# High and low weight matmuls that take turns in a column tile of a two-layer hybrid encoder

## The chip, the cores and the metric

One core of one Trainium2 chip runs the whole program in one launch. The metric is the device time of one execution in microseconds (us), the median of several runs. TensorE is called PE here, its weight loads PEld, VectorE DVE, ScalarE ACT, GpSimd POOL and SyncE SP, as in the profile.

## The reference, cut to what matters

Two layers over 256 positions of width 2048, all float32. Each layer normalises the stream, makes one large projection, feeds four mixers (A short convolution, B attention, C a scan in two directions, D a long convolution), projects each mixer back, merges them with sigmoid gates and projects once more:

```
h = rms_norm(x, norm_g)
proj = h @ w_in                       # 2048 x (13*512 + 256 + 4*2048)
ya, yb, yc, yd = mixers(split_cols(proj))
bp = einsum('bskc,kcd->bskd', stack(ya, yb, yc, yd), w_branch)
merged = sum(sigmoid(gates + b_gate) * bp, axis=2)
x = x + merged @ w_out
```

The matrices w_in, w_branch and w_out carry nearly all the arithmetic, and they are what the change touches.

## The kernel before, in words

**The weight stream.** Weights come from HBM in chunks of 128 x 1024 float32 (512 KB), 306 a layer, 612 in all, in the order of the list `STREAM` (line 90). SP loads a chunk into a `raw` buffer (`load`, line 410). ACT rounds it to a type that PE multiplies in one pass, which gives `hi` (`fetch`, line 420), and DVE subtracts, raw minus hi, which gives `lo` (`low`, line 435). There are four `raw`, three `hi` and two `lo` buffers. `chunk` (line 442) hands out the next chunk and, in program order, asks ACT for the hi two chunks ahead and DVE for the lo one chunk ahead. Both carry high priority with the scheduler. With two lo buffers, the lo of the next chunk can be written only when the last lo matmul of the chunk before this one has been done; with three hi buffers, a hi cast waits for the last hi matmul three chunks earlier.

**A column tile.** `tile_b` (line 475) makes 128 output columns for all 256 positions from two chunks, so 137 tiles a layer are 274 chunks a layer. The activations are kept split too: each operand tile is [128, 4, 2, 256], where the axis of 2 holds the high and the low part. For each chunk `wide` (line 464) makes eight matmuls with a 128x128 piece of hi against both activation parts (512 columns, into both halves of a PSUM bank) and eight with the same piece of lo against the high part alone (256 columns, into the first half). The other 32 chunks a layer belong to the branch projections; they go through `tile_branch` and `passes` (line 452), which the change leaves alone. So there are 137 x 2 x 8 x 2 layers = 4384 pairs of a hi and a lo matmul in `wide`.

**Side work between the matmuls.** The mixers are generators. After each matmul (or pair) `pump` (line 348) is called. It looks at a model clock, `now`, that each emitted matmul moves on, and emits the next step of every generator that is due, PE work on `sd` PSUM tiles included. PE's order is thus written out by the program and kept as it stands; DVE and ACT are ordered by a scheduler. Nearly all instructions are recorded at line 201, a helper, so the groups of the profile are told apart by the names of their tiles: `mg` and `mb` are PSUM banks of the weight stream, `sd` those of side work, `slab` the activation operands.

Of the kernel before, what the change touches and what calls it, by code (L numbers as in the profile page):

```python
# [211 lines left out]
class Kern:  # L212
# [250 lines left out]

    def wide(self, o, w, xs, first, last):

        nc = self.nc
        hi, lo = w
        for i, (c, x) in enumerate(xs):
            nc.tensor.matmul(o, hi[:, c * P:(c + 1) * P], x, start=first and i == 0, stop=False)
            self.pump()  # L470
        for i, (c, x) in enumerate(xs):
            nc.tensor.matmul(o[:, 0], lo[:, c * P:(c + 1) * P], x[:, 0, :], start=False, stop=last and i == len(xs) - 1)
            self.pump()

# [1039 lines left out]
```

## Time and profile before

| | |
|---|---|
| median of 3 runs | 1971.63 us (1971.6 to 1974.53) |
| the profiled execution's own time | 1974.37 us |
| its span, first to last instruction | 1972.3 us |
| mean granted TensorE clock | 0.994 |
| PE busy | 1924.5 us (98% of the span) |
| DVE busy | 1443.4 us (73%) |
| ACT busy | 1260.6 us (64%) |

Of the profiled execution 2.1 us lie outside the span, and it is 2.7 us longer than the median. Matmuls are pipelined, and the length that a record shows includes that of the pipeline; what a matmul costs in a row of matmuls is read from the distance between starts.

### The profile page before, as it was taken

The page shows a single profiled execution, that of the slowest core. Times are in us where ns is not written, and L with a number is a line of the kernel's source. Part 1 is how long each engine was busy: PE and PEld are TensorE (multiplying, and loading weights), DVE is VectorE, ACT ScalarE, POOL GpSimd, SP SyncE. Part 2 cuts the span into 40 slices and gives each one's busy share as a digit, 9 for nine tenths or more (in the row PEclk, how much of TensorE's full clock was granted, in tenths as well). Part 3 has the DMA queues.
Part 4 walks back from the last instruction along what each step waited for, and adds up shares of the span by engine and source line. Part 5 has one row for each costly group of instructions (what it writes and reads, how often), then busy time and mean ns, then how long its engine had stood idle before and what let it go on. Part 6 is the DMA issues. An engine that isn't in the chain of part 4 may idle for free.

```text
span 1972.3 us, 32350 instructions
## 1 busy us (share of the span) xinstructions
PE 1924.5 (98%) x12190; PEld 1703.6 (86%) x12190; DVE 1443.4 (73%) x2496; ACT 1260.6 (64%) x2292; POOL 71.1 (4%) x117
## 2 busy tenths in 40 slices
PE   8999999999999999999999999999999999999997
PEld 6888878898898998898888888888988889989886
DVE  7777969977788566666687679799677966565665
ACT  6677666767647776554466766776765577655544
POOL 1001010000001000000000010000001000000000
PEclk9999999999999999999999999999999999999998
DMA  7555544454565445666665555544555554465653
GB/s 249 175 169 171 164 154 144 145 168 161 169 198 171 150 150 178 201 193 216 213 191 176 176 171 163 157 149 143 176 165 179 176 178 150 152 208 196 201 184 128
DMA packets 97692, 343.17 MB, mean 174 GB/s; under 512 B 11808, under 2 KB 12192, under 8 KB 97536
## 3 DMA queue, kind: packets, MB, share of 16 engines
q1 hardware_dynamic: 93312, 331.48, 51.4%
q0 software_dynamic: 3648, 8.59, 1.8%
q8 instruction: 95, 1.56, 0.3%
q10 hardware_dynamic: 576, 1.05, 0.1%
q14 instruction: 61, 0.50, 0.1%
HBM read 332.48 MB, written 8.39 MB: 173 GB/s over the span
## 4 chain that ended last, share of the span: by engine, by line
PE 92%; DVE 6%; issue 1%; ACT 1%; DMA 0%; DVEq 0%; SPq 0%; ACTq 0%
PE mg L201 73%; PE mb L201 9%; PE sd L201 9%; DVE arena L201 3%; DVE lo L201 2%; DVE slab L201 1%; DMA arena<-xT 0%; DVE part L201 0%; DVE bdE L201 0%; ACT L175 0%; ACT arena L201 0%; ACT slab L201 0%; ACT bdE L201 0%; DVEq L1509 0%; ACT part L201 0%
## 5 line engine op out<-in xcount | busy, mean ns | idle before, releaser
L201 PE MATMUL mg<-slab,hi 128*128 128x512 f32 x4368 | 1144.3, 398 | 12.6 <-DVE slab L201 12.5
L201 DVE TENSOR_TENSOR lo<-raw,hi 128x1024 fp32r<-128x1024 f32 x612 | 747.8, 1222 | 361.6 <-PE mg L201 286.3
L201 ACT ACTIVATE hi<-raw 128x1024 fp32r<-128x1024 f32 x612 | 646.5, 1057 | 459.5 <-PE mg L201 319.5
L201 PEld LDWEIGHTS mg<-slab,hi 128*128 128x128 f32 x4368 | 781.5, 190 | 155.9 <-DVE slab L201 16.0
L201 PEld LDWEIGHTS mg<-slab,lo 128*128 128x128 f32 x4368 | 602.1, 190 | 46.0 <-issue 2.8
L201 PE MATMUL mg<-slab,lo 128*128 128x256 f32 x4368 | 635.3, 285 | 0.0
L201 DVE TENSOR_TENSOR arena<-arena 128x512 f32<-128x512 f32 (+17 forms) x390 | 165.3, 432 | 11.6 <-DMA arena<-scratch 3.5
L201 DVE SCALAR_TENSOR_TENSOR arena<-arena,par 128x256 f32<-128x256 f32 x346 | 153.1, 477 | 4.4 <-ACT arena L201 3.1
L201 PE MATMUL mb<-slab,hi 128*128 128x256 f32 (+1 forms) x1040 | 153.6, 288 | 0.0
L201 DVE TENSOR_TENSOR arena<-mg,arena 128x256 f32<-128x256 f32 x305 | 127.4, 418 | 16.0 <-ACT arena L201 10.8
L201 PEld LDWEIGHTS mb<-slab,hi 128*128 128x128 f32 x1040 | 137.2, 192 | 1.0
L201 ACT ACTIVATE arena<-arena,b_gate 128x256 f32<-128x256 f32 x128 | 64.8, 506 | 79.2 <-DVE arena L201 78.8
L201 ACT ACTIVATE arena<-arena 128x256 f32<-128x256 f32 (+4 forms) x194 | 93.5, 497 | 13.2 <-DVE arena L201 12.6
L201 ACT ACTIVATE arena<-mg 128x256 f32<-128x256 f32 x241 | 89.4, 371 | 7.6 <-PE mg L201 4.9
L201 PE MATMUL mb<-slab,lo 128*128 128x256 f32 x528 | 88.1, 287 | 0.0
L175 ACT ACT_TABLE_LOAD x62 | 79.5, 1283 | 9.5 <-PE sd L201 7.0
L201 DVE SCALAR_TENSOR_TENSOR arena<-arena,mb 128x512 f32<-128x512 f32 x64 | 43.8, 684 | 47.5 <-PE mb L201 46.3
L201 PEld LDWEIGHTS mb<-slab,lo 128*128 128x128 f32 x528 | 74.5, 193 | 0.3
L201 ACT ACTIVATE bdE<-sd 64x128 f32<-64x128 f32 x256 | 62.9, 268 | 8.3 <-PE sd L201 6.0
L201 ACT ACTIVATE arena<-sd 128x64 f32<-128x64 f32 (+4 forms) x122 | 40.2, 331 | 23.3 <-PE sd L201 21.7
L201 ACT ACTIVATE arena<-arena,par 128x256 f32<-128x256 f32 x88 | 41.2, 508 | 6.4 <-DVE arena L201 5.9
L201 PE MATMUL sd<-arena 96*128 96x256 f32 (+3 forms) x224 | 43.8, 338 | 0.9 <-DVE arena L201 0.9
(96 smaller groups left out, 1021.3 us busy)
## 6 DMA issues: line engine op xcount, KB each, us to landing
raw<-w SPq DMA_DIRECT2D x612, 512.0 KB, 3.4
arena<-xT SPq DMA_DIRECT2D x4, 512.0 KB, 8.2
scratch<-slab POOLq DMA_DIRECT2D x16, 128.0 KB, 3.0
scratch<-arena POOLq DMA_DIRECT2D x8, 256.0 KB, 4.3
arena<-xT SPq DMA_DIRECT2D x8, 256.0 KB, 3.9
x<-arena SPq DMA_DIRECT2D x8, 256.0 KB, 3.9
arena<-x SPq DMA_DIRECT2D x8, 256.0 KB, 4.3
arena<-lorab POOLq DMA_DIRECT2D x16, 96.0 KB, 3.1
```

What stands on the lines that cost most here:

```text
L175: return f(out)
L201: return f(out, *args, **kw)
```

## The change

In `wide` the second loop is gone. Each pass of the one loop that is left makes the hi matmul of a piece and then its lo matmul, and calls `pump` once behind the pair, not once behind each matmul. The number and the sizes of the matmuls are the same, `start` still stands on the first hi matmul of a tile and `stop` on its last lo matmul.

```diff
         for i, (c, x) in enumerate(xs):
             nc.tensor.matmul(o, hi[:, c * P:(c + 1) * P], x, start=first and i == 0, stop=False)
-            self.pump()
-        for i, (c, x) in enumerate(xs):
             nc.tensor.matmul(o[:, 0], lo[:, c * P:(c + 1) * P], x[:, 0, :], start=False, stop=last and i == len(xs) - 1)
             self.pump()
```

On PE, at the first chunk of the first column tile (`mg_209` is its PSUM bank, `hi_128` and `lo_130` the two parts of the chunk, `slab_106` and `slab_107` the operands), before:

```order
L201 MATMUL mg_209<-slab_106,hi_128 128x512 x4
L201 MATMUL mg_209<-slab_107,hi_128 128x512 x4
L201 MATMUL mg_209<-slab_106,lo_130 128x256 x4
L201 MATMUL mg_209<-slab_107,lo_130 128x256 x4
L201 MATMUL mg_209<-slab_108,hi_148 128x512 x4
L201 MATMUL mg_209<-slab_109,hi_148 128x512 x4
```

And with the change, the same place:

```order
L201 MATMUL mg_209<-slab_106,hi_128 128x512
L201 MATMUL mg_209<-slab_106,lo_130 128x256
L201 MATMUL mg_209<-slab_106,hi_128 128x512
L201 MATMUL mg_209<-slab_106,lo_130 128x256
L201 MATMUL mg_209<-slab_106,hi_128 128x512
L201 MATMUL mg_209<-slab_106,lo_130 128x256
L201 MATMUL mg_209<-slab_106,hi_128 128x512
L201 MATMUL mg_209<-slab_106,lo_130 128x256
```

The first lo matmul of a chunk moves from ninth place to second, and the last hi matmul from eighth to fifteenth of sixteen.

On DVE, in the convolution stage of the first layer (`lo_...<-raw_...` are the subtractions for two successive chunks, the 101st and 102nd of the layer; `arena<-arena,par_71 128x256` are taps of the long convolution of mixer D; `arena<-mg_...` is an evacuation), before:

```order
L201 TENSOR_TENSOR lo_3448<-raw_3378,hi_3414 128x1024
L201 SCALAR_TENSOR_TENSOR arena<-arena 128x256
L201 SCALAR_TENSOR_TENSOR arena<-arena,par_71 128x256
L201 TENSOR_TENSOR arena<-sd_3456,bdE_85 128x192
L201 SCALAR_TENSOR_TENSOR arena<-arena,par_71 128x256
L201 TENSOR_TENSOR bdE_83<-sd_3461,consts 64x2x64 x4
L201 TENSOR_TENSOR arena<-sd_3451,rd 128x2x64
L201 TENSOR_TENSOR arena<-sd_3451,consts 128x64
L201 TENSOR_SCALAR arena<-arena,par_71,derived_187 128x256
L201 SCALAR_TENSOR_TENSOR arena<-arena,par_71 128x256 x6
L201 TENSOR_TENSOR lo_3512<-raw_3412,hi_3446 128x1024
```

And with the change, between the subtractions for the same two chunks:

```order
L201 TENSOR_TENSOR lo_3496<-raw_3430,hi_3467 128x1024
L201 SCALAR_TENSOR_TENSOR arena<-arena,par_71 128x256
L201 SCALAR_TENSOR_TENSOR arena<-arena 128x256
L201 SCALAR_TENSOR_TENSOR arena<-arena,par_71 128x256 x2
L201 TENSOR_SCALAR arena<-arena,par_71,derived_187 128x256
L201 SCALAR_TENSOR_TENSOR arena<-arena,par_71 128x256 x3
L201 TENSOR_TENSOR part_3476<-arena,part_3476 128x512
L201 SCALAR_TENSOR_TENSOR arena<-arena,par_71 128x256 x11
L201 TENSOR_TENSOR lo_3530<-raw_3465,hi_3494 128x1024
```

Of instructions of the form SCALAR_TENSOR_TENSOR nine stand between the two subtractions before, and eighteen with the change; the small steps of the scan (`sd_...`, `bdE`) stand elsewhere. Shifts of this kind run through the whole order of ACT and DVE.

## Rows read from the trace of the kernel before

**Rows 1.** The page: busy time, share of the span and instructions of each engine, and the chain of work that ended last, by engine.

```profile
PE 1924.5 (98%) x12190; PEld 1703.6 (86%) x12190; DVE 1443.4 (73%) x2496; ACT 1260.6 (64%) x2292; POOL 71.1 (4%) x117
...
PE 92%; DVE 6%; issue 1%; ACT 1%; DMA 0%; DVEq 0%; SPq 0%; ACTq 0%
```

**Rows 2.** The page's costliest groups: line engine op, out<-in, count | busy us, mean ns of one | idle us of the engine before them, and what ended most of it.

```profile
L201 PE MATMUL mg<-slab,hi 128*128 128x512 f32 x4368 | 1144.3, 398 | 12.6 <-DVE slab L201 12.5
L201 DVE TENSOR_TENSOR lo<-raw,hi 128x1024 fp32r<-128x1024 f32 x612 | 747.8, 1222 | 361.6 <-PE mg L201 286.3
L201 ACT ACTIVATE hi<-raw 128x1024 fp32r<-128x1024 f32 x612 | 646.5, 1057 | 459.5 <-PE mg L201 319.5
...
L201 PE MATMUL mg<-slab,lo 128*128 128x256 f32 x4368 | 635.3, 285 | 0.0
```

**Rows 3.** The timeline of PE from 1000 to 1017 us, in the first tiles of the second layer, where no side work stands between: start us, length us, and the instructions merged into the row.

```profile
1000.16 2.00 PE L201 MATMUL mg<-slab,hi 128*128 128x512 f32 x8
1002.00 1.12 PE L201 MATMUL mg<-slab,lo 128*128 128x256 f32 x8
1002.96 2.00 PE L201 MATMUL mg<-slab,hi 128*128 128x512 f32 x8
...
1005.75 2.00 PE L201 MATMUL mg<-slab,hi 128*128 128x512 f32 x8
...
1008.54 2.00 PE L201 MATMUL mg<-slab,hi 128*128 128x512 f32 x8
...
1011.34 2.00 PE L201 MATMUL mg<-slab,hi 128*128 128x512 f32 x8
...
1014.13 2.00 PE L201 MATMUL mg<-slab,hi 128*128 128x512 f32 x8
...
1016.92 1.32 PE L201 MATMUL mg<-slab,hi 128*128 128x512 f32 x5
```

**Rows 4.** The timeline of weight loads (PEld) at the start of the same stretch, columns as above.

```profile
1000.05 1.70 PEld L201 LDWEIGHTS mg<-slab,hi 128*128 128x128 f32 x8
1001.78 1.13 PEld L201 LDWEIGHTS mg<-slab,lo 128*128 128x128 f32 x8
```

**Rows 5.** PE in the first hi run of rows 3, asked for in two narrow windows (the row that begins at 1000.63 begins with the third of the eight hi matmuls, the one at 1001.32 with the sixth).

```profile
1000.63 1.08 PE L201 MATMUL mg<-slab,hi 128*128 128x512 f32 x4
...
1001.32 0.39 PE L201 MATMUL mg<-slab,hi 128*128 128x512 f32 x1
```

**Rows 6.** The timeline of PE at two places where two 512-column matmuls of side work (`sd<-part,rounded`, the same type as hi) stand in a run of lo matmuls; the row after the last lo is a branch projection.

```profile
423.50 0.62 PE L201 MATMUL sd<-part,rounded 128*128 128x512 f32 x2
423.97 0.87 PE L201 MATMUL mg<-slab,lo 128*128 128x256 f32 x6
424.68 1.12 PE L201 MATMUL mb<-slab,hi 128*128 128x256 f32 x8
...
1728.16 0.62 PE L201 MATMUL sd<-part,rounded 128*128 128x512 f32 x2
1728.62 0.88 PE L201 MATMUL mg<-slab,lo 128*128 128x256 f32 x6
1729.34 1.13 PE L201 MATMUL mb<-slab,hi 128*128 128x256 f32 x8
```

**Rows 7.** The timeline of DVE in the stretch of rows 3: the six subtractions that make the lo of the chunks starting at 1002.96, 1005.75, 1008.54, 1011.34, 1014.13 and 1016.92.

```profile
1002.07 1.22 DVE L201 TENSOR_TENSOR lo<-raw,hi 128x1024 fp32r<-128x1024 f32 x1
...
1004.93 1.21 DVE L201 TENSOR_TENSOR lo<-raw,hi 128x1024 fp32r<-128x1024 f32 x1
...
1007.79 1.21 DVE L201 TENSOR_TENSOR lo<-raw,hi 128x1024 fp32r<-128x1024 f32 x1
...
1010.65 1.21 DVE L201 TENSOR_TENSOR lo<-raw,hi 128x1024 fp32r<-128x1024 f32 x1
...
1013.52 1.22 DVE L201 TENSOR_TENSOR lo<-raw,hi 128x1024 fp32r<-128x1024 f32 x1
...
1016.38 1.22 DVE L201 TENSOR_TENSOR lo<-raw,hi 128x1024 fp32r<-128x1024 f32 x1
```

**Rows 8.** Timelines at three of the other places where a chunk's lo is ready late: for each the start of the chunk's hi matmuls on PE, and the subtraction on DVE that makes its lo. The first and the last of them, and one of the two largest.

```profile
21.10 1.78 PE L201 MATMUL mg<-slab,hi 128*128 128x512 f32 x7
20.81 1.21 DVE L201 TENSOR_TENSOR lo<-raw,hi 128x1024 fp32r<-128x1024 f32 x1
...
1347.51 0.39 PE L201 MATMUL mg<-slab,hi 128*128 128x512 f32 x1
1347.33 1.22 DVE L201 TENSOR_TENSOR lo<-raw,hi 128x1024 fp32r<-128x1024 f32 x1
...
1586.22 1.55 PE L201 MATMUL mg<-slab,hi 128*128 128x512 f32 x6
1585.65 1.21 DVE L201 TENSOR_TENSOR lo<-raw,hi 128x1024 fp32r<-128x1024 f32 x1
```

**Rows 9.** The timeline of ACT in the stretch of rows 3: the cast that makes the hi of the chunk starting at 1008.54.

```profile
1002.72 1.05 ACT L201 ACTIVATE hi<-raw 128x1024 fp32r<-128x1024 f32 x1
```

**Rows 10.** The convolution stage of the first layer: a row of the timeline of DVE (three taps in a row), the subtraction behind them, and the busy time of the instructions that write or read a lo in the stretch from 310 to 370 us (PE, PEld and DVE, each with its count; then clock, DMA share and GB/s).

```profile
340.75 1.27 DVE L201 SCALAR_TENSOR_TENSOR arena<-arena,par 128x256 f32<-128x256 f32 x3
341.94 1.22 DVE L201 TENSOR_TENSOR lo<-raw,hi 128x1024 fp32r<-128x1024 f32 x1
...
310.00:370.00 60.00, 19.44 (x128) 17.81 (x128) 19.09 (x16) 1.00 0.43 144
```

## The prediction

> **What bounds the kernel now.** I read the page first: PE is busy for 98% of the span, and 92% of the chain that ended last is PE's own work [rows 1]. So the time is the sum of what PE issues, and another engine counts only where PE waits for it. The costliest groups say the same [rows 2]: in front of the 4368 hi matmuls PE stood idle for 12.6 us, in front of the lo ones for nothing, while DVE and ACT were idle for 361.6 and 459.5 us in front of their lo and hi work, mostly until PE gave a buffer back. PE is late and the others wait for it.
>
> Next I read the price of a pair where no side work disturbs it. In the second layer's first tiles six chunks begin at 1000.16, 1002.96 and so on, and the seventh at 1016.92 [rows 3]: 16.76 us for 48 pairs, or 349.2 ns a pair. Within the first chunk eight hi take 1.84 us (230 ns each) and eight lo 0.96 us (120 ns). The 4384 pairs of the column tiles make 1531 us of the 1972.3, so one nanosecond a pair is 4.4 us, more than the 3.9 us (0.2%) that a measurement can tell from no change. Two questions decide: what a pair costs when its matmuls take turns, and whether the lo is there when it is wanted.
>
> **The change part by part.** *Work.* Matmuls, weight loads, columns and transfers stay the same in number. Only order moves. The calls of `pump` halve in the column tiles, so side steps come on a grid of one pair (0.35 us) and not of one matmul. They add no work; PE is not busy for 47.8 us of the span in all [rows 1], and a tenth of that, 5 us to either side, is my estimate of what another order of side work can do. I take zero.
>
> *The switch between hi and lo.* Before, PE goes from hi to lo and back once a chunk; afterwards eight times. The nearest rows are two places where two 512-column matmuls of side work, of hi's type, stand inside a lo run, which is one more switch each way [rows 6]. From the first of them to the end of the six lo behind them it takes 1.18 us at both places. At the long-run prices, 2 x 0.230 + 6 x 0.120 is 1.18 us. The switch is free to within the 0.01 us of the rows, so I take 349.2 ns a pair still and zero for this term. The bounds: inside one hi run the first two take 0.47 us, 235 ns each (1000.16 to 1000.63), and the last three 0.68 us, 227 ns each (1001.32 to 1002.00) [rows 3, 5]. If every hi were like the last three, a pair would be 346.7 ns, 2.5 less, or 11 us off the time; if every hi were like the first two, 355, 5.8 more, or 25 us on it.
>
> *A lo that is late.* The first lo matmul stood ninth in its chunk, 1.84 us behind the first hi; now it is second, 0.23 us behind. In most chunks lo is ready long before; in some it comes between the two, which cost nothing and now does. In the stretch of rows 3 the six subtractions end 0.10, 0.16, 0.23, 0.29, 0.38 and 0.45 us later than start of chunk plus 0.23 (for the last, 1016.38 + 1.22 against 1017.15) [rows 3, 7]. DVE's period there is 2.86 us and PE's 2.79, so the lateness is carried on; a wait, once taken, moves all that follows, and the stretch costs 0.45, not the sum of 1.6. I found seven such places in the column tiles, the first worth 0.69 us, the largest 0.81, the last 0.41 [rows 8], together 3.9 us. Zero is the lower end, since a changed order may bring DVE there sooner; 14 us the upper, with the sum in place of the largest everywhere (1.6 for 0.45).
>
> *DVE's new order.* The rows of the order say that between two subtractions of the convolution stage eighteen tap-like instructions now stand, and nine before. A tap takes 0.40 us there (1.19 us for three) and sixteen chunks pass in 60 us, 3.75 us each [rows 10]. With the other two at the same price it is 20 x 0.40 + 1.22, so 9.2 us from the end of one lo to that of the next. The first can be ready at the earliest 1.2 us behind the end of the chunk two before it, the second then 10.4 behind; its chunk begins 7.5 behind, and wants it at 7.7. That is 2.7 us late. I take it once. Zero is the lower end (room that the scheduler saw may be real, PE having side work there), 8 us the upper, for three such places.
>
> *A hi buffer that comes free later.* The cast for a later chunk waits for the last hi matmul, which now ends 0.84 us nearer the end of its chunk (seven lo). What hides it is the lead: the hi cast at 1002.72 is done at 1003.77, and the subtraction that reads it starts at 1007.79 [rows 7, 9]. Four us cover it: nothing. Were that gone, the lo would be late by what is missing. ACT work that is queued behind such a cast (evacuations, scan steps) gets later by up to 0.84 us, inside the 5 us above. Loads of raw wait for lo's subtraction, not for this: nothing.
>
> Sum: 0 + 3.9 + 2.7 = 6.6 us. The profiled execution of 1974.37 us is 2.7 us over the median; it would become 1981.0, and the median of 1971.6 becomes **1978.2 us**.
>
> **The rivals.** *Every hi finds its load done (1967 us or less).* A weight load starts with the matmul before it: lo's first at 1001.78, when the eighth hi begins [rows 4], 0.22 us ahead of its own matmul at 1002.00. Taking turns puts each lo's load under a long matmul, and each run's slow first hi may vanish: the -11 above with the waits gives 1967.2, without them 1960.6. Against it: in rows 6 the inserted pair takes 0.47 and 0.46 us, not 0.45. Chance 0.26.
>
> *Both loads under the long matmul (1938 us).* If PE fetched two loads ahead, the lo would cost only its columns, half of 227, so a pair 340 ns: 9.2 less, 40 us off. For it speaks only that lo's 120 ns exceed half of hi's. Against it: no load in rows 4 starts earlier than the matmul in front of it. Chance 0.06. [...]
>
> *The switch costs (2003 us).* Each hi follows a lo, as the first in a run does, and stays at 235 ns; nothing settles: 25 + 6.6. For it: the inserted 512-column matmuls were at 233 to 235 ns. Against it: the lo behind them were then cheaper (0.71 us for six, 118 ns) and gave it back. Chance 0.14.
>
> *Nothing to measure (1971.6 us).* The scheduler, which sees the earlier need, brings each lo in time, and the switch is free. For it: DVE's 361.6 idle us in front of lo. Chance 0.16.
>
> **How the numbers follow.** The forecast has 0.38, and so the time. Slower by over 0.2%: 0.30 from it (its waits shrink below 3.9 us in some cases), 0.14 from the dear switch, 0.04 from the rest: 0.48. Faster: 0.17 from the settled hi, 0.06 from the hidden loads, 0.04 from shifts of side work: 0.27. Same: 0.25. The range leaves out the hidden loads and about half of the dear switch, and goes from 1958 (settled hi, no waits, side work a little luckier) to 2000. The forecast's own range, with its bounds on waits and side work, is 1967 (no waits, 5 off) to 1999 (14 and 8 and 5 on).
>
> **What would show it.** Right: in the timeline around the second layer's start a pair of 349 ns with hi near 233 and lo near 117, and short stops in front of lo matmuls, released by DVE's lo, 2 to 10 us in all, some in the convolution stage. Wrong: a pair that is 2 ns or more off 349.2 in undisturbed chunks (then the rivals on the switch have it), no idle time in front of lo, or a new large wait in front of side work on `sd`, which my 5 us would not hold.

## The result, and the profile after

| | before | after |
|---|---|---|
| median of the runs on one chip | 1973.08 us (4 runs) | 1999.41 us (4 runs, 1997.64 to 2003.08) |
| after / before, 95% interval | | 1.0130 (1.0118 to 1.0142) |
| profiled execution: own time, span | 1974.37, 1972.3 us | 1997.64, 1995.6 us |

The change costs 26 us. Forecast were 6.6, in a range that ended at 2000: the sign is right, the size is four times what was forecast, and the time lies in the range by 0.6 us.

The page of the kernel after, busy times, and the groups that answer to [rows 1, 2], with the weight loads of lo added:

```profile
PE 1936.5 (97%) x12190; PEld 1706.5 (86%) x12190; DVE 1456.7 (73%) x2496; ACT 1270.9 (64%) x2292; POOL 71.6 (4%) x117
...
L201 PE MATMUL mg<-slab,hi 128*128 128x512 f32 x4368 | 1588.5, 405 | 10.6 <-DVE slab L201 10.5
L201 PE MATMUL mg<-slab,lo 128*128 128x256 f32 x4368 | 1230.2, 282 | 1.9 <-DVE lo L201 1.7
...
L201 PEld LDWEIGHTS mg<-slab,lo 128*128 128x128 f32 x4368 | 830.6, 190 | 10.0 <-DVE lo L201 4.0 <-issue 3.8
```

PE is busy for nearly the same share and still bounds the kernel. Stops in front of lo exist now and are small: 1.7 us in the row of the matmuls, 4.0 in that of their loads. So the 23.3 us by which the span grew are mostly not there. (The busy time of a group is a union; with hi and lo in turns the two groups overlap, so 1588.5 and 1230.2 can't be set against [rows 2]. One tile's 16 pairs carry the name `mb`, so the groups count 4368 and not 4384.)

The timeline of PE in the undisturbed stretch, answering to [rows 3]:

```profile
1000.23 0.40 PE L201 MATMUL mg<-slab,hi 128*128 128x512 f32 x1
1000.46 0.28 PE L201 MATMUL mg<-slab,lo 128*128 128x256 f32 x1
1000.58 0.40 PE L201 MATMUL mg<-slab,hi 128*128 128x512 f32 x1
...
1006.23 0.40 PE L201 MATMUL mg<-slab,hi 128*128 128x512 f32 x1
...
1006.94 0.39 PE L201 MATMUL mg<-slab,hi 128*128 128x512 f32 x1
1007.93 0.38 PE L201 MATMUL mg<-slab,lo 128*128 128x256 f32 x1 [0.60 <-DVE lo L201]
```

From 1000.23 to 1006.23 there are 17 pairs in 6.00 us, 353 ns each, against 349.2 (over all plain pairs of the trace it is 351.0, below). At 1006.94 PE meets a lo that is late, as forecast for this stretch: 0.99 us from hi to lo and not 0.23, so 0.76 us once, where 0.45 was expected. The weight loads still lead by one matmul, as in [rows 4]:

```profile
1000.24 0.19 PEld L201 LDWEIGHTS mg<-slab,lo 128*128 128x128 f32 x1
1000.47 0.19 PEld L201 LDWEIGHTS mg<-slab,hi 128*128 128x128 f32 x1
```

The place of [rows 10], in the kernel after; DVE between the two subtractions, then PE:

```profile
343.26 1.22 DVE L201 TENSOR_TENSOR lo<-raw,hi 128x1024 fp32r<-128x1024 f32 x1
...
346.23 1.27 DVE L201 SCALAR_TENSOR_TENSOR arena<-arena,par 128x256 f32<-128x256 f32 x3
347.42 0.69 DVE L201 TENSOR_TENSOR part<-arena,part 128x512 fp32r<-128x512 f32 x1
348.02 3.26 DVE L201 SCALAR_TENSOR_TENSOR arena<-arena,par 128x256 f32<-128x256 f32 x8
```

```profile
344.06 0.28 PE L201 MATMUL mg<-slab,lo 128*128 128x256 f32 x1
346.65 0.50 PE L201 MATMUL sd<-part,rounded 128*128 128x512 f32 x1 [2.30 <-ACT part L201]
348.17 0.60 PE L201 MATMUL sd<-part,rounded 128*128 128x512 f32 x1 [1.02 <-DVE part L201]
```

The row of taps is there, but what it keeps waiting is not lo: PE stands in front of side work, 3.3 us in two stops, 2.30 for a `part` (a rounded operand of a side matmul) that ACT makes late and 1.02 for one that DVE makes among the taps. While PE stands, DVE works the taps off, and PE does not stop for the second lo.

Side work is where most of the time went. For each profiled execution I added up the distances between starts on PE. A plain pair is the mean distance behind a hi plus that behind a lo, over those that no side work follows, that lie at full clock and that are at most 45 ns over 230 and 119. "Side work" is all time from a weight matmul's plain end to the next weight matmul where side work stands between; PE's work in it is the same in every kernel, so differences are stops; the profile's own waits agree (PE idle in front of side matmuls: 22.9 us before, 34.1 after). "Halved clock" is what weight matmuls took more than their plain price while the granted clock stood at half. In us:

| | hi + lo = pair, ns | 4384 pairs | side work | halved clock | short stops of some 86 ns | longer stops in the weight stream | all else |
|---|---|---|---|---|---|---|---|
| before | 230.4 + 118.9 = 349.3 | 1531.2 | 189.8 | 5.9 | 22.0 | 17.3 | 206.1 |
| after | 234.0 + 117.0 = 351.0 | 1538.9 | 200.9 | 8.4 | 24.5 | 17.2 | 205.7 |
| difference | 1.7 | 7.7 | 11.1 | 2.5 | 2.5 | -0.1 | -0.4 |

So a third is the pair and half is stops in front of side work. The halved clock came with stops too. Apart from the last microseconds (from 1962.0 us before and from 1986.8 after) the granted clock fell to half (0.50) four times before and six times after, for 3.4 us each but once, after, for 6.8, each time during a stop of PE or soon after one, though not behind every stop (before, PE stood 2.38 us until 605.40, and the clock stayed at 1.00). It also differs between executions of one kernel: the mean was 0.993 to 0.996 in those of the kernel before, which took 1976.6 to 1971.9 us. A few us in that column, read from one execution each, are therefore no effect of an edit by themselves.

The largest stops in front of side work, on PE after, with the idle time and its releaser in brackets (the one at 1239.38 stands in front of transposes of the second layer's attention, the others in front of matmuls on working memory that DVE has just written):

```profile
594.17 1.22 PE L201 MATMUL sd<-arena,consts 128*128 128x256 f32 x2 [3.81 <-DVE arena L201]
...
1239.38 1.08 PE L201 MATMUL sd<-consts,arena 128*128 128x128 f32 x4 [5.95 <-issue]
...
1587.80 1.22 PE L201 MATMUL sd<-arena,consts 128*128 128x256 f32 x2 [4.85 <-DVE arena L201]
```

The same three groups of matmuls on PE before; in front of the first two PE does not stand:

```profile
590.52 0.60 PE L201 MATMUL sd<-arena,consts 128*128 128x256 f32 x2
...
1226.78 0.78 PE L201 MATMUL sd<-consts,arena 128*128 128x128 f32 x4
...
1574.06 0.70 PE L201 MATMUL sd<-arena,consts 128*128 128x256 f32 x2 [2.40 <-DVE arena L201]
```

### The profile page after: what moved, and what is told of

It reads as the page before. It is cut to its first block, busy times and chain, and to the rows that moved or that the text cites. A ratio compares the mean times of both kernels' runs of the same rounds, so it can differ in the third digit from the quotient of the medians.

```text
span 1995.6 us, 32314 instructions
## 1 busy us (share of the span) xinstructions
PE 1936.5 (97%) x12190; PEld 1706.5 (86%) x12190; DVE 1456.7 (73%) x2496; ACT 1270.9 (64%) x2292; POOL 71.6 (4%) x117
## 5 line engine op out<-in xcount | busy, mean ns | idle before, releaser
L201 PE MATMUL mg<-slab,hi 128*128 128x512 f32 x4368 | 1588.5, 405 | 10.6 <-DVE slab L201 10.5
L201 PE MATMUL mg<-slab,lo 128*128 128x256 f32 x4368 | 1230.2, 282 | 1.9 <-DVE lo L201 1.7
L201 PEld LDWEIGHTS mg<-slab,hi 128*128 128x128 f32 x4368 | 825.6, 189 | 201.4 <-DVE slab L201 11.5
L201 PEld LDWEIGHTS mg<-slab,lo 128*128 128x128 f32 x4368 | 830.6, 190 | 10.0 <-DVE lo L201 4.0
L201 DVE TENSOR_TENSOR arena<-arena 128x512 f32<-128x512 f32 (+18 forms) x390 | 166.3, 432 | 11.0 <-ACT arena L201 5.0
L201 ACT ACTIVATE slab<-arena 128x512 fp32r<-128x512 f32 (+1 forms) x64 | 33.0, 518 | 22.3 <-DVE arena L201 22.1
```

Source lines behind the costliest of these rows:

```text
L201: return f(out, *args, **kw)
```

## The experiments

Four theories. **Switch**: a pair costs more when hi and lo alternate. **Late lo**: the lo wanted 1.6 us earlier stops PE. **Blocked cast**: the hi buffer that comes free later delays ACT's casts and what is queued behind them. **Places**: side work falls to other places of PE's order, and the scheduler orders DVE and ACT anew, which makes stops whatever hi and lo do. Ratios are to runs of the kernel before on the same chip (its medians were 1973.1 to 1975.0 us); the columns after them are read from one profiled execution each.

### First set: the order and how often side work is asked

**Turns, side work asked after every matmul.**

```diff
 (in the loop of the change)
             nc.tensor.matmul(o, hi[...], x, ...)
+            self.pump()
             nc.tensor.matmul(o[:, 0], lo[...], x[:, 0, :], ...)
             self.pump()
```

> Hi and lo take turns as in the change, but the side work is asked after every matmul, as before, not once a pair. Switch theory: the pair stays at 351.0 ns (349.3 before), worth 7.5 us, whatever the side work does. Coarse-grid theory: the rest of the 26 us, 16 us of stops in front of side work and of halved clock, goes; time about 1981 us. Placement theory (any new order of the side work makes its own stops, the grid is not to blame): 1975 to 2000 us with the pair at 351.0. Late-lo theory: no change against the kernel after, 1999 us, with waits in front of lo.

**Runs of eight, side work asked after every second matmul.**

```diff
 (in both loops of the kernel before)
-            self.pump()
+            if i % 2:
+                self.pump()
```

> The order before (eight hi, then eight lo), with the side work asked after every second matmul, so as often a chunk as in the change. Switch theory: the pair is at 349.3 ns. Coarse-grid theory: 16 us more than before, about 1989 us. Placement theory: 1970 to 1992 us, and the stops stand at other places than in either kernel. Late-lo theory: as before, 1973 us.

**Runs of four.**

```diff
+        for g in (xs[:4], xs[4:]):   # xs numbered; inside: the two loops of before, over g
```

> Four hi, four lo, four hi, four lo, the side work asked after every matmul: two switches each way a chunk in place of one or eight. If each switch costs the same, 1.7 ns over seven more switches gives 349.3 + 0.2 = 349.5 ns a pair; if a run needs some five hi to settle, hi near 232 and lo near 118, 350.5 ns. Time by the switch alone 1974 to 1978 us; placement adds anything from 0 to 20.

**Turns with lo three pieces behind.**

```diff
+        for j in range(n + 3):
+            if j < n:     # hi matmul of piece j, then self.pump()
+            if j >= 3:    # lo matmul of piece j - 3, then self.pump()
```

> Hi and lo take turns, but lo lags three pieces behind (three hi, then a hi and a lo in turn, then three lo), the side work asked after every matmul: the first lo is wanted 0.9 us behind the first hi, not 0.23. Late-lo theory: the stops in front of lo (1.9 us and what they push) go, and the time falls well below the kernel after. Switch theory: pairs at about 350.5 ns (five of eight in turns). Placement theory: 1973 to 2000 us whatever lo does.

| | median us | ratio (95%) | pair ns | side work us | halved clock us |
|---|---|---|---|---|---|
| turns, asked each | 2095.47 | 1.0612 (1.0594 to 1.0629) | 350.9 | 297.6 | 19.4 |
| runs of eight, asked each second | 2080.16 | 1.0537 (1.0519 to 1.0555) | 349.3 | 289.8 | 23.4 |
| runs of four | 1986.05 | 1.0057 (1.0042 to 1.0072) | 350.4 | 197.2 | 6.8 |
| turns, lo lags three | 2100.24 | 1.0634 (1.0618 to 1.0650) | 351.0 | 297.2 | 23.9 |

No theory had 100 us. The same 105 us of the first layer, busy times of PE, PEld, DVE, ACT, POOL, then clock, DMA share and GB/s, in the first of these and in the kernel before:

```profile
740.00:845.00 105.00, 72.72 (x465) 62.70 (x464) 30.89 (x76) 56.88 (x170) 1.73 (x3) 0.74 0.18 52
```

```profile
740.00:845.00 105.00, 105.00 (x658) 94.72 (x657) 65.44 (x85) 58.78 (x91) 0.00 (x0) 1.00 0.58 188
```

PE is idle for a third of the stretch, and 52 GB/s of weights come in place of 188: the second scan of the layer runs alone with no weight matmuls to cover it. In PE's order its second half began behind 2599 of the layer's 5152 weight matmuls before, 2572 in the change and 2570 with runs of four; in the three slow kernels it begins behind 3397 to 3404, and its last `bdX` matmuls (the inverses) behind 3898 to 3912 in place of 3106. The program holds the scan back until its working memory has room; that on another grid it lost this room to later work is my reading of the program and not shown. So these three tell nothing of lateness or of blocked casts. They do tell the price of a pair: 350.9 and 351.0 in turns, 349.3 in runs, whatever the side work does, as the switch theory said (for the lag it had 350.5). The coarse grid as such (a rival of mine) they leave open, since the scan swamps it. Runs of four, with no uncovered scan, cost 11 us: 5 by the pair, and 7.4 more than before in side work.

### Second set: side work held in its place

To part order and places, `wide` was written as sixteen slots: the weight matmul in a slot comes from one list, the advance of the model clock and the call of `pump` from another.

```diff
+        for s, ((part, i), (cost, ask)) in enumerate(zip(order, model)):
+            ...                      # the hi (part 0) or lo (part 1) matmul of piece i
+            self.now = t + cost      # t: the clock before it (self.due, set after it, is not shown)
+            if ask:
+                self.pump()
```

With `model` that of eight hi and then eight lo, every side instruction on PE stands behind the same count of weight matmuls as before; with `model` that of pairs, as in the change. DVE and ACT are still ordered by the scheduler. The lists (H and L with the piece's number):

```
turns, old places:       H0 L0 H1 L1 ... H7 L7                 model: runs
runs, new places:        H0 ... H7 L0 ... L7                   model: pairs
lag of three, old places: H0 H1 H2 H3 L0 H4 L1 ... H7 L4 L5 L6 L7   model: runs
serpentine, old places:  H0..H7 L0..L7, next chunk L0..L7 H0..H7    model: runs
early lo, old places:    H0 L0 H1 ... H7 L1 ... L7             model: runs
late hi, old places:     H0 ... H6 L0 ... L6 H7 L7             model: runs
```

> Hi and lo take turns, but the model clock is moved on as in the order before, so every side instruction on PE stands at the same count of weight matmuls as before. Switch theory: 351.0 ns a pair, 7.5 us, and with up to 4 us of waits in front of lo 1980 to 1985 us; stops in front of side work as before. Placement theory (two thirds of the 26 us come from where side work stands): the same 1980 to 1985. Against it: if the turns themselves make DVE and ACT late for side work, the time is 1995 to 2000 us although side work stands where it stood.

> Eight hi, then eight lo, with every side instruction at the count of weight matmuls at which it stands in the change. Switch theory and placement theory: 349.3 ns a pair, but the stops in front of side work of the change: 16 us more than before, 1987 to 1992 us. If the turns themselves make the stops: as before, 1973 to 1977 us.

> Lo lags three pieces behind hi, side work where it stood before. The first lo of a chunk is wanted 0.9 us behind the first hi, not 0.23. Switch theory: 350.9 ns a pair as it was measured in turns with this lag, 7 us. Late-lo theory: 2 to 4 us less than with turns at the same places; if lateness costs nothing, the same as there.

> First chunk of a tile eight hi then eight lo, second chunk eight lo then eight hi, side work where it stood before: runs of sixteen, half the switches of before. Switch theory: the 20 ns that a switch each way costs a chunk fall to 10, 348.1 ns a pair, 5 us less, 1968 us with nothing else. Late-lo theory: every second chunk wants lo at its start, as in the change: up to 4 us of waits, 1972 us. Both: about 1970 us.

> Each chunk: one hi, one lo, then seven hi, then seven lo; side work on PE where it stood before. The first lo is wanted second, as in the change, but the last hi stands ninth, nearly where it stood. Late-lo theory (the early need for lo brings the stops): 1985 to 1992 us. Blocked-cast theory (ACT's casts wait longer for a hi buffer, and ACT work queued behind them is late): as before, 1975 to 1979 us, of which two more switches a chunk may be 1 to 5.

> Each chunk: seven hi, seven lo, then the last hi and the last lo; side work on PE where it stood before. The hi buffer comes free as late as in the change, the first lo is wanted eighth. Blocked-cast theory: 1985 to 1992 us, with stops in front of side work that ACT released. Late-lo theory: as before, 1975 to 1979 us.

| | median us | ratio (95%) | pair ns | side work us | halved clock us | last hi stands |
|---|---|---|---|---|---|---|
| turns, old places | 1994.26 | 1.0099 (1.0082 to 1.0115) | 350.8 | 199.1 | 7.5 | 15th |
| runs, new places | 1992.47 | 1.0091 (1.0076 to 1.0106) | 349.1 | 202.1 | 12.1 | 8th |
| lag of three, old places | 1981.62 | 1.0036 (1.0023 to 1.0049) | 350.8 | 194.6 | 3.2 | 12th |
| serpentine, old places | 1990.62 | 1.0083 (1.0066 to 1.0099) | 348.5 | 210.3 | 4.7 | 8th, 16th |
| early lo, old places | 1980.07 | 1.0032 (1.0020 to 1.0044) | 350.8 | 191.0 | 4.0 | 9th |
| late hi, old places | 1989.72 | 1.0081 (1.0066 to 1.0096) | 350.6 | 196.0 | 10.2 | 15th |

Several expectations were missed. The serpentine came 20 us above its 1970. Turns at old places, at 1994, lie above the 1980 to 1985 of the switch and the places and at the edge of the 1995 to 2000 of turns that make DVE and ACT late. The lag gained 12.6 us on them and not 2 to 4.

*Late lo falls.* With lo wanted second and the hi buffer free at the ninth place, the time is up by 6.0 us, which is the price of its pairs (1.5 ns x 4384 = 6.6); PE's idle time put down to a late lo is 0.8 us. *The coarse grid is not needed:* turns at old places ask for side work after every matmul and cost 19 us. *The late hi buffer counts, at the old places.* Late hi has lo wanted eighth and nearly the same pair, yet costs 9.7 us more than early lo; a lag of three, whose last hi stands twelfth, is like early lo, and turns at the same places, where it stands fifteenth, cost 12.6 us more than the lag. The serpentine, whose every second chunk ends with hi, has a cheaper pair (-0.8 ns) and loses it many times over in front of side work. At these places PE's idle time in front of side matmuls for a `part` of ACT follows the place of the last hi (waited for: us in total, times, longest us): 1.2 us before, 1.7 with early lo (below, first line), 3.9 with the lag, 6.4 with late hi (second line), 9.0 with turns, 8.1 with the serpentine.

```profile
PE sd L201 <- ACT part L201: 1.7, 3, 0.6
```

```profile
PE sd L201 <- ACT part L201: 6.4, 8, 1.3
```

That is not the whole price. The profiled executions of early lo and late hi are 12.2 us apart, and of this 5.0 are side work, 6.2 halved clock and some 3 longer stops in the weight stream, with 1 less in the pairs. The execution of late hi is the slowest of its four, with the lowest clock (0.991 against 0.993 and 0.994), so the 6.2 are partly chance.

How a late buffer becomes a stop is seen at one place, behind 679 weight matmuls, and again in the second layer behind 5831. PE with early lo, then with late hi:

```profile
142.88 0.50 PE L201 MATMUL sd<-part,rounded 128*128 128x512 f32 x1
143.61 0.50 PE L201 MATMUL sd<-part,rounded 128*128 128x512 f32 x1 [0.23 <-DVE part L201]
```

```profile
149.16 0.50 PE L201 MATMUL sd<-part,rounded 128*128 128x512 f32 x1 [1.24 <-ACT part L201]
149.88 0.50 PE L201 MATMUL sd<-part,rounded 128*128 128x512 f32 x1 [0.22 <-DVE part L201]
```

And ACT ahead of it, with early lo, then with late hi:

```profile
137.51 1.06 ACT L201 ACTIVATE hi<-raw 128x1024 fp32r<-128x1024 f32 x1 [1.13 <-PE mg L201]
138.48 0.62 ACT L201 ACTIVATE arena<-arena 128x512 f32<-128x512 f32 x1
139.11 1.28 ACT L175 ACT_TABLE_LOAD   x1
...
142.19 0.63 ACT L201 ACTIVATE part<-arena 128x512 fp32r<-128x512 f32 x1
142.73 0.72 ACT L201 ACTIVATE arena<-arena 128x512 f32<-128x512 f32 x2
```

```profile
143.17 0.63 ACT L201 ACTIVATE arena<-arena 128x512 f32<-128x512 f32 x1 [1.44 <-DVE arena L201]
143.71 1.05 ACT L201 ACTIVATE hi<-raw 128x1024 fp32r<-128x1024 f32 x1
144.65 0.72 ACT L201 ACTIVATE arena<-arena 128x512 f32<-128x512 f32 x2
145.39 1.28 ACT L175 ACT_TABLE_LOAD   x1
...
148.48 0.63 ACT L201 ACTIVATE part<-arena 128x512 fp32r<-128x512 f32 x1
```

With early lo the hi cast is done before the chain to `part` begins, and from the square (138.48) to `part` it takes 3.7 us. With late hi the chain takes 5.3, and PE waits for it: the cast stands inside it, and so do two other activations (the row at 144.65) that early lo makes behind `part`. So about 0.9 of the 1.6 us are the cast's. It is not that ACT stood blocked at the cast, as the theory had it: no idle time stands in front of it, the order of ACT is another. PE's stop at this place is 1.51 us with turns at old places, 0.52 with the lag, and none before or with the serpentine. The two places are 2.5 us of late hi's price; for the rest the cast is argued, not shown.

*Places count as well.* The order of before with the side work where the change has it costs 18 us, and no pair of it is dearer; in the profiled execution 12.3 us are side work and 6.2 halved clock. (How much of it the coarser grid of calls brings is not parted from the places.) Its largest stops are those of the kernel after, with eight hi and eight lo around them:

```profile
594.27 0.70 PE L201 MATMUL sd<-arena,consts 128*128 128x256 f32 x2 [3.62 <-DVE arena L201]
...
1237.98 1.09 PE L201 MATMUL sd<-consts,arena 128*128 128x128 f32 x4 [6.32 <-issue]
```

In all, eight groups of side matmuls have a stop of more than 1.7 us in the kernel after, 25.4 us together. In front of the same groups PE stands 25.8 us here, 6.8 before and 7.8 with turns at old places. So the stops of the kernel after are those of its places. And with the side work at the new places, turns add 6.9 us (1992.47 to 1999.41; by the ratios 7.7), no more than their pairs cost. The change as it was made is thus accounted for by places (18 us) and pair (7.7), 25 of the 26 us; the late hi buffer, worth some 10 us at the old places, adds nothing here that shows.

The stop of 6 us shows how a place makes one. The kernel after puts scan steps (`bdR`) between the last score matmuls of attention (`kz`) and the transposes that PE then waits for:

```profile
1224.99 1.02 PE L201 MATMUL sd<-kz,arena 128*128 128x512 f32 x2
...
1229.03 0.60 PE L201 MATMUL sd<-bdR,slab 128*128 128x128 f32 x4
```

ACT serves the scan first, and its activation on the scores, whose result is transposed, starts 12.5 us behind the score matmuls (5.0 us before), after a wait that the profile puts down to a DMA:

```profile
1230.77 1.01 ACT L201 ACTIVATE bdE<-sd 64x128 f32<-64x128 f32 x4
...
1237.52 0.47 ACT L201 ACTIVATE arena<-sd,arena 128x256 f32<-128x256 f32 x1 [2.40 <-DMA scratch<-arena]
```

Runs at new places and turns with the other number (next set) have the same order and stops of 6.3 and 5.5 us. Before, at the old places, with runs of four and in runs with the other number no scan step stands between, and PE does not stand.

### Third set: one number of the model clock

```diff
-                    k.now += max(0.12, n * 0.4445e-3)
+                    k.now += max(0.119, n * 0.45e-3)
```

in the kernel before and in the changed one.

> The order before (eight hi, eight lo, side work asked after every matmul) with one number of the model clock changed, the price of a weight matmul column from 0.4445 to 0.45 ns: no matmul of a chunk changes places, but side work falls elsewhere and the scheduler orders DVE and ACT anew. Placement theory (any other place of the side work than that of before costs something): 1980 to 1992 us, with the pair at 349.3 ns. If only turns cost: 1973 to 1977 us.

> The change with the same one number of the model clock changed. The pair stays at 351.0 ns. Placement theory: the stops in front of side work come out differently from those of the change, the time between 1985 and 2010 us. If the stops belong to the turns: 1997 to 2002 us, with the large stops near 590, 1233 and 1583 us still there.

| | median us | ratio (95%) | pair ns | side work us |
|---|---|---|---|---|
| runs, other number | 1979.33 | 1.0029 (1.0018 to 1.0040) | 349.3 | 194.7 |
| turns, other number | 1993.92 | 1.0104 (1.0086 to 1.0121) | 351.0 | 195.8 |

A change that alters no matmul's neighbour in a chunk costs 5.3 us through places alone, a fifth of what the change costs (a little under the 1980 to 1992 expected). In turns the other number gains some 5 us on the kernel after (the two intervals of the ratio just touch). The stop of 6 us in the second layer's attention stays (5.5 us), the one near 1583 stays and grows (6.2 us), the one near 590 is gone (0.8 us), and a stop of 3.8 us stands at 601. So how much places cost hangs on a number; that any other place costs something was so in each of the kernels here, but it is no rule.

## Why the prediction was right in sign, and where it failed

- **What bounds the kernel**: right. PE bounds both (busy for 98% and 97% of the span).
- **The switch, taken at zero**: wrong. It is 1.7 ns a pair, 7.7 us. Where runs of four switch once more each way, a chunk costs 9 ns more (1.1 ns x 8), which the 0.01 us of [rows 6] could not show; the lo run there came to 0.71 and 0.72 us for six (118 and 120 ns). In the stretch named as the sign, the pair is 353 ns, 4 off, so that sign of being wrong came true. The bound of 5.8 ns held, as did hi near 233 and lo near 117 (234.0 and 117.0). Nor is the price one per switch, as I reckoned: 348.5 ns with half a switch each way a chunk, 349.3 with one, 350.4 to 350.8 with two, 350.8 to 351.0 with more. Read by place in a run of the kernel before, hi costs 233, 234, 229, 232 and 230 ns and 227 from the sixth on, lo 114, 119 and then 120. In turns every hi stays at the dear start of a run and lo gives back only a part. The expectation for runs of four had this as its second case (hi near 232, lo near 118, 350.5 a pair), and that is what they gave.
- **The late lo, 3.9 us**: the stops are there, 1.7 to 4.0 us, one of them in the stretch named (1007.93 above). They did not lengthen the kernel: longer stops in the weight stream came to 17.3 us before and 17.2 after, since others, in front of hi, shrank (12.6 to 10.6 us). With early lo 0.8 us is left of this term.
- **DVE's new order, 2.7 us once**: the row of taps is there, its victim is another. PE stopped 3.3 us in front of side work, 1.0 of it for the `part` that stands among the taps; the term had looked at lo alone.
- **The hi buffer that comes free later, nothing**: I looked at who reads hi (four us of lead) and left ACT's other work inside 5 us. With side work at the old places the late buffer costs about 10 us, halved clock included; at the new places, so in the change itself, turns cost no more than their pairs.
- **Side work moved, 5 us to either side, taken at zero**: the step that failed most. A tenth of PE's idle time was no measure of it: the new places alone cost 18 us in the order of before, by stops mostly where PE had not stood. The parts are not additive: places, turns at the old places and their pairs together are more than 26. That a stop in one place gives DVE and ACT time to be ready at the next would explain it, and is argued.
- **Rivals.** The dear switch (2003 us) came nearest in time and has a third of the cause. Against it the prediction reads the inserted matmuls of [rows 6] as 233 to 235 ns; by the rows (0.47 and 0.46 us for two) they are 235 and 230. Settled hi and hidden loads are refuted by 351.0 ns; loads still start with the matmul in front of them (a load of lo at 1000.24 us, the hi matmul there at 1000.23). That there would be nothing to measure is refuted by the 26 us. Of what was said would prove the forecast wrong, the large wait in front of `sd` came true as well.

So the direction came out right by luck: the forecast's own two waits bring hardly any of it, and what brings it, places and pair, had been taken at zero. That the time is inside the range is luck too, since its upper end was added up from the bounds of those waits and 5 us of side work, with half of the dear switch.

## What to carry to other kernels

Where the order of PE is written out and other engines serve it, price a reordering by everybody whose buffers it frees later, and look for what else waits on the engine that fills them, not only for the reader of the buffer (here this showed only with the side work held in its place). Where a planner places side work by a model clock, a change of order is two changes; test each without the other (by feeding the planner the old clock, or the new clock with the old order), since here the two did not add up. And a planner with a memory limit can fall off a cliff: three harmless-looking edits here cost 100 us.

## What the runs showed of the hardware that was not expected

- Matmuls of 512 and 256 columns with a weight load each did not simply add here. In runs of eight a pair takes 349.3 ns, in turns 351.0; hi 4 ns more, lo 2 ns less. A run of hi settles at 227 ns from the sixth on, a run of lo at 120 from the third. What in PE does this is open.
- Some 260 to 290 short stops of about 86 ns stand in the weight stream (22.0 us before, 24.5 after), and some 150 to 200 in the three kernels with the uncovered scan. What makes them is open; between before and after they differ by 2.5 us.
- In the three kernels with the uncovered scan the granted clock fell to half again and again while PE kept standing still (in the first of them the mean was 0.74 in the 105 us above, and PE idle for a third; over whole executions of the three it was 0.963 to 0.969, and 0.993 to 0.996 in those of the kernel before), and the weight matmuls under it took 19 to 24 us more than at full clock, against 6 before.
